# Weights of a decoder block's FFN through shared buffers, and the first three down tiles in another order

## The chip, the cores and the metric

One NeuronCore of a Trainium2 chip runs the whole kernel. The time is device microseconds of one execution, the median of several; the profile is that of one execution, with times counted from the start of its span. Engines are named PE (TensorE), DVE (VectorE), ACT (ScalarE), POOL (GpSimd) and SP (SyncE, which issues the DMAs here).

## The reference, cut to what matters

One layer of a decoder, fp32, 1024 tokens of 1024 channels:

```python
h = x
h = h + token_mixer(rms_norm(h, norm_mix))              # three branches, merged, @ w_mix_out
h = h + cross_attention(rms_norm(h, norm_ca), mem_n)    # 4 heads, 256 memory tokens
hn = rms_norm(h, norm_ffn)
u = causal_dwconv(hn @ ffn_up, ffn_conv_w) + ffn_conv_b # 2 x 2816 columns, width 3 over tokens
gate, val = split(u, 2)
h = h + (silu(gate) * val) @ ffn_down                   # 2816 x 1024
out = rms_norm(h, norm_final)
```

## The kernel before, in words

Every fp32 factor of a product is split into a high and a low part, and a product is three matmuls: high by high, high by low, low by high. A weight or an activation therefore passes four steps before PE can use it: a load into a raw buffer, a cast on ScalarE (high), a subtraction on DVE or GpSimd (low), and then the matmuls. `split_tile` (L233) does this for a weight, in two halves, `pair` (L1483) for a tile of hidden values.

The stream h lives in SBUF as eight tiles h0 to h7 of 128 tokens by 1024 channels. The program runs in stages. The token mixer ends with the merge: `accumulate` (L1079) multiplies activations by rows of a weight for each of the eight token tiles and adds the result to h on DVE (L1097); with `add=False` ScalarE copies it into h instead (L1100). Then `norm_T` (L202) normalises h for the cross-attention: a square with a row sum on ScalarE (L191), some short steps, a scale on DVE (L219), transposes on PE (L225), cast and subtraction (L230, L231). `q_proj` (L1160), `attend` (L1177) and `accumulate` follow for each of four heads.

The FFN's up projection uses a fast scheme for 2 x 2 blocks: the token tiles, even and odd, and the halves of the channels form the blocks. `operands` (L1321) builds the block operands b11, b21, b22 and t1 to t4 from the transposed tiles; `put` (L1306) writes an operand's high and low part, and the low parts of t1, t3 and t4 are GpSimd's (`POOL_T`). For each of 22 hidden tiles f, the loop at L1439 loads four raw weight blocks a11, a12, a21, a22 of the gate and value columns (`raw`, L1411, six raw buffers), forms four sums of them on GpSimd (`wsum`, L1417), splits seven weights (`parts`, L1423), and runs seven products of 12 matmuls (`product`, L1343; 84 matmuls instead of 96). Sums of products make the gate's and the value's columns in four tiles of h (`places`, L1362): even f use h0, h4, h1, h5, odd f h2, h6, h3, h7, since h itself was stored to HBM in `normed` (L1295). The convolution (`conv`, L1431) takes one step on ScalarE and two on DVE, then SiLU (L1461) and a multiply on GpSimd (L1463), and the hidden tile is stored (L1464). The first products of tiles 0 and 1 use weights made ahead, during the cross-attention (`early_parts`, L1285); hidden tile 0 and down row 0 are fetched ahead by `early_pair` (L1399) when f is 14.

The down projection starts at L1502: hidden 0 by down row 0 for the eight token tiles in the order 4, 0, 1, 5, 3, 7, 6, 2, written into h; then hidden 1 and 2 for all tiles, with the residual h loaded and added on GpSimd (`residual`, L1478); then groups of 3, 3, 3, 4 and 4 hidden tiles, and the final norm and the store of the output with the last.

A scheduler puts the instructions of each engine into one order ahead of time, by program order and the offsets of `tc.high_priority`. Each engine works through its order in turn, so a waiting instruction holds those behind it; SP's queue of DMA issues too. SBUF comes from pools, opened and closed like a stack, and a tile in a place that another tile held waits for that tile's last reader. PSUM is two buffers `pd` (1024 columns) and four `pq` (512).

## Time and profile before

| | |
|---|---|
| runs | 2342.14, 2349.14, 2349.61 us; median 2349.14 |
| profiled execution | 2349.42 us, its span 2347.7 us |
| PE busy | 2213.9 us, 94% of the span |
| DVE, ACT, POOL busy | 1443.4, 896.5, 593.6 us |
| mean granted clock of TensorE | 0.975 |

The span is the time from the first to the last instruction, and 1.7 us of the execution lie outside it. A row of a timeline gives the start in the span, the length, the engine, the line, the operation and the tiles written and read; in brackets stands how long the engine had been idle and what ended that. A row that ends in "x3" holds three instructions. The granted clock is TensorE's share of full speed in a stretch. The merge ends at 1345 us, the up loop's last product at 2074 us.

### The profile page before, as it was taken

Reading aid. Unit: us, or ns where it says so; the run is one execution under the profiler, and the core shown is the slowest. Engines: PE = TensorE matmul, PEld = TensorE weight load, DVE = VectorE, ACT = ScalarE, POOL = GpSimd, SP = SyncE. Lnnn points to the kernel's source line nnn. Section 1 sums busy time; section 2 is a strip of 40 time slices with the busy share of each in tenths; the row PEclk is TensorE's granted clock in tenths of the full one; section 3 lists DMA queues with packets and bytes.
Section 4 is the critical chain, followed back from the end, with each engine's and each line's share of the span. In section 5 each row is a group of like instructions: output and inputs, shape, how many; then the busy total and the mean of one; then the engine's idle time right before and its main releaser. Section 6 shows DMA issues by size and latency. Waiting matters only on the chain. (4 is left out here: it accounts for less than half of the span.)

```text
span 2347.7 us, 30015 instructions
## 1 busy us (share of the span) xinstructions
PE 2213.9 (94%) x11635; PEld 1839.8 (78%) x11635; DVE 1443.4 (61%) x1948; ACT 896.5 (38%) x1494; POOL 593.6 (25%) x501
## 2 busy tenths in 40 slices
PE   6999999999999999999999989997899999978998
PEld 5888888878888888887877777875678888867887
DVE  7575555673245245447866565548788888866535
ACT  6644233343434244445521253226444444341212
POOL 2124322222323233221121100004644444313000
PEclk9999989999999999999999999998899999989999
DMA  4334623532211222116664120112222222154311
GB/s 159 117 108 169 204 84 116 146 89 83 81 54 46 90 64 62 64 64 211 217 233 173 63 63 27 32 36 99 91 80 90 82 89 81 55 187 140 116 32 72
DMA packets 232223, 238.93 MB, mean 102 GB/s; under 512 B 35347, under 2 KB 190225, under 8 KB 231057
## 3 DMA queue, kind: packets, MB, share of 16 engines
q1 hardware_dynamic: 232081, 237.02, 31.2%
q8 instruction: 91, 1.49, 0.3%
q14 instruction: 51, 0.42, 0.1%
HBM read 170.92 MB, written 66.06 MB: 101 GB/s over the span
## 5 line engine op out<-in xcount | busy, mean ns | idle before, releaser
L244 ACT CAST wh<-wr 128x512 fp32r<-128x512 f32 x266 | 156.9, 620 | 357.9 <-PE pd L1095 114.7
L245 POOL TENSOR_TENSOR wl<-wr,wh 128x512 fp32r<-128x512 f32 x128 | 177.7, 1405 | 260.4 <-ACT wh L244 246.7
L1097 DVE TENSOR_TENSOR h<-pd,h 128x1024 f32<-128x1024 f32 x120 | 146.3, 1222 | 149.9 <-PE pd L1095 149.8
L284 PE MATMUL pd<-xn_hi,wh 128*128 128x512 f32 x576 | 227.7, 395 | 0.0
L285 PE MATMUL pd<-xn_lo,wh 128*128 128x512 f32 x576 | 225.0, 391 | 0.0
L288 PE MATMUL pd<-xn_hi,wl 128*128 128x512 f32 x576 | 178.4, 391 | 0.0
L266 PE MATMUL pd<-xn_lo,wh 128*128 128x512 f32 x384 | 151.9, 396 | 0.0
L265 PE MATMUL pd<-xn_hi,wh 128*128 128x512 f32 x384 | 151.8, 395 | 0.0
L245 DVE TENSOR_TENSOR wl<-wr,wh 128x512 fp32r<-128x512 f32 x138 | 102.5, 765 | 64.2 <-ACT wh L244 63.1
L938 DVE TENSOR_TENSOR_SCAN B<-B 128x128 f32<-128x128 f32 (+3 forms) x64 | 86.9, 1358 | 84.5 <-POOL B L935 84.1
L1428 DVE TENSOR_TENSOR wp<-ws,wp 128x512 fp32r<-128x512 f32 x88 | 119.8, 1362 | 13.9 <-ACT wp L1427 13.3
L288 PEld LDWEIGHTS pd<-xn_hi,wl 128*128 128x128 f32 x576 | 108.0, 188 | 23.6 <-POOL wl L245 0.2
L285 PEld LDWEIGHTS pd<-xn_lo,wh 128*128 128x128 f32 x576 | 108.4, 188 | 19.8
L284 PEld LDWEIGHTS pd<-xn_hi,wh 128*128 128x128 f32 x576 | 108.2, 188 | 19.5
L269 PE MATMUL pd<-xn_hi,wl 128*128 128x512 f32 x384 | 121.4, 394 | 0.0
L1346 PE MATMUL pq<-t,wp 128*128 128x512 f32 x264 | 103.8, 393 | 16.5 <-ACT wp L1427 16.5
L1463 POOL TENSOR_TENSOR h<-h,h 128x1024 f32<-128x1024 f32 x22 | 56.4, 2564 | 203.3 <-ACT h L1461 171.3
L955 DVE TENSOR_TENSOR al<-pq,ah 128x512 fp32r<-128x512 f32 x80 | 54.6, 688 | 85.6 <-ACT ah L954 85.2
L1427 ACT CAST wp<-ws 128x512 fp32r<-128x512 f32 x88 | 54.4, 618 | 129.5 <-POOL ws L1420 73.9
L1348 PE MATMUL pq<-t,wp 128*128 128x512 f32 x264 | 103.7, 393 | 0.0
L1347 PE MATMUL pq<-t,wp 128*128 128x512 f32 x264 | 103.7, 393 | 0.0
L954 ACT CAST ah<-pq 128x512 fp32r<-128x512 f32 x80 | 46.9, 588 | 145.9 <-PE pq L950 145.6
(420 smaller groups left out, 5812.8 us busy)
## 6 DMA issues: line engine op xcount, KB each, us to landing
wr<-in_w_comb_dram SPq DMA_DIRECT2D x124, 256.0 KB
raw<-in_ffn_up_dram SPq DMA_DIRECT2D x88, 256.0 KB
gate_d<-ft SPq DMA_DIRECT2D x24, 512.0 KB
hid_d<-h SPq DMA_DIRECT2D x22, 512.0 KB
t<-hid_d SPq DMA_DIRECT2D x21, 512.0 KB
wr<-in_ffn_down_dram SPq DMA_DIRECT2D x38, 256.0 KB
wr<-in_ca_wkv_dram SPq DMA_DIRECT2D x32, 256.0 KB
ft<-gate_d SPq DMA_DIRECT2D x16, 512.0 KB
```

Of the source, the lines that this page charges most:

```text
L244: s_.copy(hi[:, sl], raw)
L245: (v_ if lo_e == "dve" else g_).tensor_tensor(lo[:, sl], raw, f32(hi[:, sl]), ALU.subtract)
L265: pe.matmul(o, wh(k), xh(k, h), start=k == 0, stop=False)
L266: pe.matmul(o, wh(k), xl(k, h), start=False, stop=False)
L269: pe.matmul(o, wl(k), xh(k, h), start=False, stop=k == nk - 1)
L284: pe.matmul(o, wh(k), xh(k, h), start=k == 0, stop=False)
L285: pe.matmul(o, wh(k), xl(k, h), start=False, stop=False)
L288: pe.matmul(o, wl(k), xh(k, h), start=False, stop=k == nk - 1)
L1097: v_.tensor_tensor(h[i], ps, h[i], ALU.add)
L1346: pe.matmul(ps, wh[:, k, :], xh[:, k, :], start=k == 0, stop=False)
L1347: pe.matmul(ps, wh[:, k, :], xl[:, k, :], start=False, stop=False)
L1428: v_.tensor_tensor(lo, src, f32(hi), ALU.subtract)
```

## The change

The early weights no longer have a pool of their own. The first up weights of tiles 0 and 1, and later hidden 0 and down row 0, go through `wc`, the pool of the query projection's weights, which is opened first and kept to the end. Behind the norm a pool `raw` of four raw tiles is opened, kept to the end too; the pools `wo` and `co` are opened behind it, where they stood ahead of the norm before. In the up loop five of six raw weight blocks take a tile of `raw`, every sixth one of two buffers of the loop's own pool, and the four of tile 0 are loaded during the cross-attention. `normed` uses its result tile as scratch, of which there are two instead of three. The operands of the last token tiles and the first products alternate in another way. A hidden tile is stored one tile later, behind the next tile's first sums. In the down projection `soon` fetches hidden 1, 2 and down rows 1, 2 in halves through `raw`; tiles 4, 0, 1, 5 take hidden 0, then 1 and 2; then tiles 3, 7, 6, 2 take all three. The residual comes with the next group, of two hidden tiles, and the raw halves of all later down rows pass through `raw`.

```diff
+SOON = 250
-GROUPS = (2, 2, 3, 3, 3, 4, 4)
+GROUPS = (2, 3, 3, 3, 4, 4)
...
-        def split_tile(pl, src, shape, lo_e="dve", tag="w", parts=2, rbufs=3):
+        def split_tile(pl, src, shape, lo_e="dve", tag="w", parts=2, rbufs=3,
+                       rpool=None):
...
-                raw = pl.tile([P, n] + list(shape[2:]), F32, name=tag + "r", bufs=rbufs)
+                if rpool:
+                    raw = rpool.tile([P, 4, P], F32, name="raw").rearrange("p a t -> p (a t)")
+                else:
+                    raw = pl.tile([P, n] + list(shape[2:]), F32, name=tag + "r", bufs=rbufs)
...
-        early = pool(est, "early")
+        early = wp = pool(est, "wc", 2)
         with ExitStack() as st:
-            wo = pool(st, "wo", 2)
-            op = pool(st, "co", 2)
             s3 = ExitStack()
-            wp = pool(s3, "wc", 2)
...
                     norm_T(np_, h, gb, hh, hl, 1)
+            rawp = pool(est, "raw", 4)
+            wo = pool(st, "wo", 2)
+            op = pool(st, "co", 2)
...
-            first = [[early_parts(kh, f) for kh in range(2)] for f in range(2)]
+            rawn, wu = [], []
+
+            def raw(kh, c):
+                rawn.append(0)
+                if len(rawn) % 6 < 5:
+                    t = rawp.tile([P, 4, P], F32, name="raw")
+                else:
+                    t = wu[0].tile([P, 4, P], F32, name="raw", bufs=2)
...
+            first = []
+            for f in range(2):
+                w = split_tile(early, up[:, :, f * P:(f + 1) * P], [P, KD, P], lo_e="pool", rbufs=1)
+                first.append([(w[0][:, k:k + 4, :], w[1][:, k:k + 4, :]) for k in (0, 4)])
+            raw0 = raws(0)
...
-                xs = np_.tile([P, D], F32, name="xs", bufs=3)
+                xs = np_.tile([P, D], F32, name="xs", bufs=2)
+                rs = rms(np_, h[i], xs)
...
-            done = []
-            for f in range(2):
-                done.append(even_products(*first[f]))
-                for _ in range(1 + f):
-                    operands(*todo.pop(0))
+            done = [even_products(*first[0])]
             operands(*todo.pop(0))
-            for f in range(2):
-                even_sums(f, *done[f])
+            done.append(even_products(*first[1]))
+            operands(*todo.pop(0))
+            even_sums(0, *done[0])
+            operands(*todo.pop(0))
+            even_sums(1, *done[1])
+            operands(*todo.pop(0))
...
-                t = wp.tile([P, 4, P], F32, name="raw", bufs=6)
...
+            def store(f):
+                if f >= 0:
+                    dma(hid_d[f], places(f)[0])
...
-                a11, a12 = raw(0, f), raw(1, f)
-                a21, a22 = raw(0, NF + f), raw(1, NF + f)
+                a11, a12, a21, a22 = raws(f) if f else raw0
                 if f >= 2:
                     even_sums(f, *even_products(parts(a11), parts(a12)))
+                store(f - 1)
...
-                dma(hid_d[f], t0)
...
+            def soon(src, tag):
+                hi, lo = tag
+                for sl in (slice(0, 512), slice(512, 1024)):
+                    raw = rawp.tile([P, 4, P], F32, name="raw").rearrange("p a t -> p (a t)")
+                    with tc.high_priority(offset=SOON + 300):
+                        dma(raw, src[:, sl])
+                    with tc.high_priority(offset=SOON):
+                        s_.copy(hi[:, sl], raw)
+                        v_.tensor_tensor(lo[:, sl], raw, f32(hi[:, sl]), ALU.subtract)
+                return hi, lo
...
+            tt = top_tile()
+            tops = [(tt[:, 2 * x], tt[:, 2 * x + 1]) for x in range(4)]
+            w3 = [(d0[0], d0[1])]
+            for x, k in enumerate((1, 2)):
+                w3.append([soon(src[k], tops[2 * x + y]) for y, src in enumerate((hid_d, down))])
+            last()
+            a3, b3 = [w[0] for w in w3], [w[1] for w in w3]
+            accumulate(None, a3[:1], b3[:1], add=False, order=(4, 0, 1, 5))
+            accumulate(None, a3[1:], b3[1:], order=(4, 0, 1, 5))
+            accumulate(None, a3, b3, add=False, order=(3, 7, 6, 2))
...
-                if gi == 0:
-                    ws = [pair(None, hp2.tile([P, T], F32, name="t", bufs=3), down[k], x[1])
-                          for k, x in zip(ks, tiles[2:])]
-                    accumulate(None, [d0[0]], [d0[1]], add=False, order=(4, 0, 1, 5, 3, 7, 6, 2))
-                    gbf = bcast_row(hp2, A["norm_final"][None, :], "gbf")
-                    accumulate(None, acts, ws, after=residual)
-                else:
-                    accumulate(wp, acts, [down[k] for k in ks],
-                               after=final if f == NF else None)
+                accumulate(wp, hidden(ks, tiles), [down[k] for k in ks],
+                           after=final if f == NF else residual if gi == 0 else None, rpool=rawp)
```

Lines of the kernel after the change are 1 to 27 higher for the same statement (L1097 becomes L1103, L1100 L1106, L1420 L1427, L1309 L1327, L1434 and L1436 L1441 and L1443). The orders below are read out of both programs; tiles carry their numbers.

DVE at the end of the merge. h6 and h7 are token tiles whose last sum (L1097, now L1103) ends the merge; ss, rs, rt and xs belong to the norm of a tile, mk and mv to the key and value tiles of the first head. Before:

```order
L1097 TENSOR_TENSOR h6_10567<-pd_11420,h6_10567 128x1024
L1097 TENSOR_TENSOR h7_10568<-pd_11434,h7_10568 128x1024
L192 TENSOR_SCALAR ss_11477<-ss_11477 128x1
L192 TENSOR_SCALAR ss_11488<-ss_11488 128x1
L196 RECIPROCAL rs_11480<-rt_11481 128x1
L196 RECIPROCAL rs_11491<-rt_11492 128x1
L197 SCALAR_TENSOR_TENSOR rt_11481<-rs_11480,ss_11477 128x1
```

With the change:

```order
L1196 TENSOR_TENSOR mv_lo_11834<-kvr_11831,mv_hi_11833 128x512
L200 TENSOR_TENSOR rs_11617<-rs_11617,rt_11618 128x1
L232 TENSOR_TENSOR hn_lo_11461<-pq_11626,top_11460 128x4x128
L232 TENSOR_TENSOR hn_lo_11461<-pq_11633,top_11460 128x4x128
L220 SCALAR_TENSOR_TENSOR xs_11651<-h6_10567,rs_11617,gb_11465 128x1024
L1103 TENSOR_TENSOR h7_10568<-pd_11434,h7_10568 128x1024
L1190 TENSOR_TENSOR mk_lo_12262<-kvr_12259,mk_hi_12261 128x512
L232 TENSOR_TENSOR hn_lo_11461<-pq_11653,top_11460 128x4x128
L232 TENSOR_TENSOR hn_lo_11461<-pq_11660,top_11460 128x4x128
```

The norm's steps stood behind all eight sums; now those of h0 to h6 stand between and ahead of them, and h7's sum comes behind the subtractions of mk and mv.

POOL at the FFN's start. ws are the weight sums of up tile 0, t1, t3 and t4 operands (their low parts), L1340 (now L1358) a difference of two blocks in h. Before:

```order
L1340 TENSOR_TENSOR h4_10565<-h4_10565,h5_10566 128x512
L1309 TENSOR_TENSOR t41_13319<-h4_10565,t40_13318 128x4x128
L1309 TENSOR_TENSOR t11_13313<-h6_10567,t10_13312 128x4x128
L1309 TENSOR_TENSOR t31_13317<-h7_10568,t30_13316 128x4x128
L1340 TENSOR_TENSOR h6_10567<-h6_10567,h7_10568 128x512
L1420 TENSOR_TENSOR ws_13826<-raw_13822,raw_13824 128x512
L1420 TENSOR_TENSOR ws_13828<-ws_13826,raw_13818 128x512
L1309 TENSOR_TENSOR t41_13319<-h6_10567,t40_13318 128x4x128
L1420 TENSOR_TENSOR ws_13848<-raw_13818,raw_13822 128x512
```

With the change:

```order
L1427 TENSOR_TENSOR ws_13817<-raw_13349,raw_13351 128x512
L1427 TENSOR_TENSOR ws_13819<-ws_13817,raw_13345 128x512
L1427 TENSOR_TENSOR ws_13839<-raw_13345,raw_13349 128x512
L1327 TENSOR_TENSOR t41_13318<-h4_10565,t40_13317 128x4x128
L1327 TENSOR_TENSOR t11_13312<-h6_10567,t10_13311 128x4x128
L1358 TENSOR_TENSOR h6_10567<-h6_10567,h7_10568 128x512
L1327 TENSOR_TENSOR t31_13316<-h7_10568,t30_13315 128x4x128
L1427 TENSOR_TENSOR ws_13892<-raw_13347,ws_13819 128x512
L1327 TENSOR_TENSOR t41_13318<-h6_10567,t40_13317 128x4x128
```

The first two weight sums moved ahead of four operand steps, of h4, h6 and h7, the third ahead of five.

DVE where the up loop ends. L1360 (now L1378) are the last sums of up tile 21, L1434 and L1436 (L1441, L1443) its convolution in h2 and h6, L1493 and L245 (L1505, L250) low parts of hidden tiles and down rows, L1103 a sum into h. Before:

```order
L1360 TENSOR_TENSOR h3_10564<-pd_16856,h6_10567 128x4x128
L1434 SCALAR_TENSOR_TENSOR h2_10563<-h3_10564,prf_103,h2_10563 128x1023
L1436 SCALAR_TENSOR_TENSOR h2_10563<-h3_10564,prf_103,h2_10563 128x1022
L1493 TENSOR_TENSOR top_16929<-t_16930,top_16929 128x1024
L1493 TENSOR_TENSOR top_16929<-t_16934,top_16929 128x1024
L1493 TENSOR_TENSOR top_16929<-t_16938,top_16929 128x1024
L1493 TENSOR_TENSOR top_16929<-t_16942,top_16929 128x1024
L1434 SCALAR_TENSOR_TENSOR h6_10567<-h7_10568,prf_103,h6_10567 128x1023
L245 TENSOR_TENSOR wl_17160<-wr_17162,wh_17161 128x512
L1436 SCALAR_TENSOR_TENSOR h6_10567<-h7_10568,prf_103,h6_10567 128x1022
L245 TENSOR_TENSOR wl_17160<-wr_17166,wh_17161 128x512
```

With the change:

```order
L1378 TENSOR_TENSOR h3_10564<-pd_16847,h6_10567 128x4x128
L250 TENSOR_TENSOR wl_17135<-raw_17137,wh_17136 128x512
L250 TENSOR_TENSOR wl_17135<-raw_17141,wh_17136 128x512
L1441 SCALAR_TENSOR_TENSOR h2_10563<-h3_10564,prf_103,h2_10563 128x1023
L1443 SCALAR_TENSOR_TENSOR h2_10563<-h3_10564,prf_103,h2_10563 128x1022
L1441 SCALAR_TENSOR_TENSOR h6_10567<-h7_10568,prf_103,h6_10567 128x1023
L1443 SCALAR_TENSOR_TENSOR h6_10567<-h7_10568,prf_103,h6_10567 128x1022
L1505 TENSOR_TENSOR al_17125<-t_17123,ah_17124 128x1024
L1103 TENSOR_TENSOR h4_10565<-pd_16985,h4_10565 128x1024
L250 TENSOR_TENSOR wl_17145<-raw_17151,wh_17146 128x512
L1103 TENSOR_TENSOR h0_10561<-pd_16999,h0_10561 128x1024
```

The four convolution steps stand together, and the low parts of hidden 1, 2 and down 1, 2 (L1516) stand ahead of these rows, among the earlier sums of up tile 21.

## Rows read from the trace of the kernel before

**Rows 1.** Windows of 50 us: stretch, length, busy PE, PEld, DVE, ACT, POOL (instructions), PEclk, DMA.

```profile
1350.00:1400.00 50.00, 42.49 (x208) 34.93 (x209) 34.27 (x73) 25.80 (x53) 0.00 (x0) 0.89 0.25 74
1600.00:1650.00 50.00, 28.64 (x140) 23.25 (x138) 38.59 (x67) 29.51 (x58) 26.50 (x20) 0.81 0.22 74
1650.00:1700.00 50.00, 44.49 (x179) 35.56 (x178) 42.98 (x43) 22.39 (x32) 27.62 (x18) 0.92 0.33 103
1750.00:1800.00 50.00, 50.00 (x222) 41.42 (x221) 44.73 (x47) 22.32 (x30) 21.86 (x12) 1.00 0.25 82
2050.00:2100.00 50.00, 40.67 (x163) 31.85 (x162) 27.73 (x31) 22.73 (x26) 7.94 (x2) 0.88 0.46 163
2100.00:2150.00 50.00, 41.39 (x168) 32.49 (x167) 35.15 (x27) 11.02 (x14) 21.31 (x8) 0.95 0.57 189
```

**Rows 2.** Timeline of PE, 1350 to 1361: start, length, line, operation, [idle before].

```profile
1351.34 3.43 PE L225 MATMUL pq<-ident,xs 128*128 128x128 f32 x16 [6.10 <-DVE ss L192]
1356.37 1.06 PE L225 MATMUL pq<-ident,xs 128*128 128x128 f32 x8 [1.60 <-DVE xs L219]
1360.52 1.94 PE L225 MATMUL pq<-ident,xs 128*128 128x128 f32 x8 [3.08 <-DVE ss L192]
```

**Rows 3.** Timeline of ScalarE at the end of the merge.

```profile
1345.27 1.06 ACT L191 ACTIVATE junk<-h 128x1024 f32<-128x1024 f32 x1 [27.52 <-PE pd L1095]
```

**Rows 4.** Timeline of PE, 1649 to 1669, the first up tiles.

```profile
1649.38 0.79 PE L1346 MATMUL pq<-t,wp 128*128 128x512 f32 x1 [16.50 <-ACT wp L1427]
1668.71 0.77 PE L1346 MATMUL pd<-b,wp 128*128 128x512 f32 x1 [5.50 <-DVE h L1360]
```

**Rows 5.** Timeline of GpSimd (POOL), 1646 to 1650.

```profile
1646.07 1.26 POOL L1420 TENSOR_TENSOR ws<-raw 128x512 f32<-128x512 f32 x1
1648.63 1.27 POOL L1309 TENSOR_TENSOR t<-h,t 128x512 fp32r<-128x512 f32 x1
```

**Rows 6.** Timeline of PE, 2090 to 2136, the down projection begins.

```profile
2091.33 0.79 PE L1091 MATMUL pd<-ew 128*128 128x512 f32 x1 [6.61 <-ACT h L1100]
2096.45 0.80 PE L1091 MATMUL pd<-top 128*128 128x512 f32 x1 [2.19 <-ACT h L1100]
2135.96 0.75 PE L1091 MATMUL pd<-wh,ah 128*128 128x512 f32 x1 [4.99 <-DVE h L1097]
```

**Rows 7.** Timelines of SP (issues) and ScalarE, 1375 to 1379.

```profile
1375.14 0.34 SPq L1180 DMA_DIRECT2D kvr<-mk_d  x1
1378.17 0.62 ACT L1183 CAST mk_hi<-kvr 128x512 fp32r<-128x512 f32 x1 [0.25 <-DMA kvr<-mk_d]
```

**Rows 8.** Timelines of ScalarE, DVE and GpSimd, last up tile.

```profile
2085.31 1.24 ACT L1432 ACTIVATE h<-h,prf 128x1024 f32<-128x1024 f32 x1
2088.39 1.28 DVE L1436 SCALAR_TENSOR_TENSOR h<-h,prf,h 128x1022 f32<-128x1022 f32 x1
2089.81 5.54 POOL L1463 TENSOR_TENSOR h<-h,h 128x1024 f32<-128x1024 f32 x1 [25.30 <-DVE h L1436]
```

**Rows 9.** Timelines of DVE, GpSimd and ScalarE, 2109 to 2135.

```profile
2122.84 1.23 DVE L1097 TENSOR_TENSOR h<-pd,h 128x1024 f32<-128x1024 f32 x1 [1.49 <-PE pd L1095]
2126.71 8.07 DVE L1493 TENSOR_TENSOR top<-t,top 128x1024 fp32r<-128x1024 f32 x3
2119.93 13.76 POOL L1481 TENSOR_TENSOR h<-h,hr 128x1024 f32<-128x1024 f32 x5 [0.40 <-DMA hr<-h_d]
2109.47 0.62 ACT L244 CAST wh<-wr 128x512 fp32r<-128x512 f32 x1 [2.40 <-DMA wr<-in_ffn_down_dram]
```

**Rows 10.** Lines of GpSimd, 1740 to 2050; then timelines, ScalarE and PE.

```profile
L1420 POOL TENSOR_TENSOR ws<-raw 128x512 f32<-128x512 f32 x32 | 53.8, 1682 | 1.3
L1463 POOL TENSOR_TENSOR h<-h,h 128x1024 f32<-128x1024 f32 x17 | 40.8, 2402 | 156.9 <-ACT h L1461 156.9
2047.83 0.63 ACT L1427 CAST wp<-ws 128x512 fp32r<-128x512 f32 x1 [3.04 <-POOL ws L1420]
2071.16 0.39 PE L1346 MATMUL pd<-b,wp 128*128 128x512 f32 x1
```

53 lines of the change are left out of this document (23 added, 30 removed).

## The prediction

> **What bounds the kernel now.** I read the table of windows first [rows 1]. Its PE column is the engine's busy time in 50 us: from 1750 to 2050 every window is full at a granted clock of 1.00, so nothing in the up loop can be won but fewer matmuls, and the change keeps their number. PE is short in three places only: 42.5 of 50 us from 1350 (the norm ahead of cross-attention), 28.6 and 44.5 from 1600 (the operands of the FFN), 40.7 and 41.4 from 2050 (from the up loop into the down projection). The granted clock is lower in the same windows (0.81 to 0.95, means of stretches at 2.4 and at 1.2 GHz), and each of them holds gaps, so an idle microsecond there costs a little more than itself. Then the PE timeline of each place, for the gaps in brackets and the engine that ended them, and after it the timeline of that engine.
>
> At the norm PE waits 6.10, 1.60 and 3.08 us [rows 2] (two smaller gaps add 1.5), because ScalarE's first square starts only at 1345.27, after the last matmul of the merge, having been idle for 27.52 us [rows 3], while the sums of h0 to h6 were ready one by one, every 2.72 us, before that. At the FFN's start PE waits 16.50 us for a weight's cast and 5.50 us for a sum [rows 4]; GpSimd has one chain there, and the first two weight sums stand at its end, at 1646.07 [rows 5]. At the down projection the gaps are 6.61, 2.19 and 4.99 us [rows 6], with three of 0.8 to 1.5 us between.
>
> **Part 1, the norm.** The norm's buffers no longer lie where they must wait for the merge, so its squares, scales and transposes move in between the last eight sums. What it can give: the 10.8 us of [rows 2] less the tail of h7 (its sum, square, scale and transposes, some 2 us of them before PE can start), 9 us. What it can cost: DVE has the sum (1.23 us [rows 9]), the scale of about the same length and five short instructions for every tile that PE finishes in 2.72 us; that is slightly over PE's pace, and the last sums slip by some 5 us in all. The order also puts the subtractions of the key and value tiles ahead of h7's sum, and such a load took 3.0 us from its issue at 1375.14 to its cast at 1378.17 [rows 7]. If that load is waited for in full where nothing covers it, the place loses 3 us. Going down the new order with these durations I find h7's last transposes at about 1371.5, where the key load, which waits for them today, went out at 1375.14 [rows 7]. I take **-4 us** (between +3 and -9).
>
> **Part 2, the FFN's start.** On GpSimd the first two weight sums now stand ahead of four operand steps that they followed, the third ahead of five. The product that waited 16.50 us needs the first two sums, its cast and the operand t2; what it gains is bounded by the four steps that are passed, at 1.27 us each [rows 5], so some 5 us and, with 2 us of the second gap, 7. But the low part of t3's last piece now comes after all three (3.8 us), and t3's product stands right behind t2's on PE. The work that GpSimd has in all is the same. So part of the 16.50 goes and part comes back at the next product; at worst the three sums delay t3 by 3 us more than t2 gains. The 5.50 us gap is the same chain one tile on, and moves with it. Going down the order: PE restarts at about 1647.4 instead of 1649.38, and the second gap is about 1 us shorter. I take **-3 us** (+3 to -7). The first up weights, loaded through the query projection's buffers and with raw tiles ahead, I cost at nothing: they are hidden by the attention of the last head, in which PE was not waiting for a load; without that cover a load of 3 us [rows 7] would show once.
>
> **Part 3, the down projection.** Output tiles 3, 7, 6 and 2 are written where the last up tile (f=21) has its sums. Today the product with hidden 0 runs over all eight tiles, 48 matmuls or 10.9 us at 0.227 us (some 220 in a full window [rows 1]), and then stands: f=21's value half gets its convolution late, behind casts (ScalarE 2085.31, DVE until 2089.67), and GpSimd's multiply, which frees h6, runs from 2089.81 for 5.54 us [rows 8], where it takes 2.40 in the loop [rows 10]. The loss: from the end of the last up product (2071.16 plus 12 matmuls, 2073.9 [rows 10]) to 2135.96 there are 62.1 us, in which 169 matmuls ran, 38.3 us; so 23.8 us went, 18 of it in gaps and the rest at the lower clock.
>
> After the change tiles 4, 0, 1, 5 take hidden 0, 1 and 2 first: 24 + 48 matmuls, 16.3 us, to 2090.2. The order places the four convolution steps together (4 x 1.25 us), so they end at about 2082, the multiply follows, 2.4 to 5.5 us, and the store of hidden 21 is needed only for tile 2, the last. So 3, 7, 6, 2 find their places free, and the 72 matmuls left end at about 2107.8 (1 us of gaps). Today the same 144 were done at about 2125.4 (the gap of 4.99 began at 2130.97 and the next group had run 24 matmuls, 5.6 us). That is 17.6 us.
>
> What is late next is the residual: it still comes in GpSimd's five adds of the next group. Beside them DVE's three subtractions took 8.07 us, 2.7 each instead of 1.23, and the adds 13.76, and behind these stands the sum that PE waited 4.99 us for [rows 9, 6]. The Trainium skill ("GPSIMD Engine Reference", section Specifications) says that GpSimd's SBUF interface is shared with VectorE, and that an instruction with two SBUF inputs contends. By it the gap stays, since the subtractions read both operands from SBUF, and the part gives 17.6; were it only late data, the gap would go with earlier loads and the part would give 22.6. The trace agrees with the rule: beside the same adds DVE's sums, which read one operand from PSUM, kept their 1.23 us [rows 9]. I leave the gap where it is, and take off one more of the size of those that a sum of DVE ended before (1.5 us), since the four weights of that group now come through four raw tiles. I take **-16 us**: at most -23 (all that was lost but one microsecond), at least -8 (the gaps after 2100, 8.6 us, come a second time).
>
> The eight half loads of hidden 1, 2 and down 1, 2, with 8 casts and 8 subtractions (0.6 and 0.7 us), stand before f=21's sums on ScalarE and DVE, 5 us on each. Their cover: the last weight of the up loop was cast at 2047.83 and used at 2071.16 [rows 10], so both engines have 23 us in which PE needs only evacuations, and the tiles go in after 2060, when the last product that reads that place is over. Without the cover f=21's sums, and with them PE, would be late by up to those 5 us. The deferred store of a hidden tile frees SP's queue and costs nothing while nothing reads it for 20 us.
>
> **Sum.** -4 - 3 - 16 = -23 us, on the profiled execution's 2349.42 us: **2326.4 us**. (That execution is 0.28 us above the median of the three runs.) 7 us, 0.3%, is about what can be told from no change.
>
> **Rivals.**
> 1. *The down projection keeps half its gaps* (16%). For: the weights now come in 256 KB halves through four raw tiles; ScalarE's order has up to six casts ahead of the copy that empties PSUM for tile 3, and a cast that waits for its load holds that copy. Today such casts waited up to 2.40 us each for their loads [rows 9]. Against: these loads go out 20 us earlier. Price: -8 there, and -1 each in the other places: 2339. (The Trainium skill, "DMA: Bandwidth & Descriptors", section Bandwidth, wants transfers of 1 MiB or more, which speaks against cutting 512 KB in two; no run here shows the loss.)
> 2. *The raw ring starves the up loop* (6%), the case that ends slower. Place: 1750 to 2050. Now six raw tiles, each in its turn; then five of six come from four tiles, and the second pair of a tile can be loaded only when the last weight sum of the tile before has read its own. The round is then a load (3.0 [rows 7]), four weight sums (4 x 1.68) and the multiply (2.40) [rows 10], 12.1 us. It decides once it is over the 19.03 us of a tile, so if loads or waits in SP's queue add 7 us. At 20.5 us, 20 tiles lose 29 us, and with the gains of the other parts the time is 2355. Against: the 7 us, and weights that lie ready 23 us ahead.
> 3. *The change doesn't do what it says* (7%): norm and FFN give back what they win (the slipped sums, the passed operands), and the down projection saves only the 6.61: 2343 to 2350, no change.
> 4. *Everything moves by its upper bound* (9%): -9, -5, -22: 2313.
>
> **How the numbers follow.** The forecast has 62%, by itself 2317 to 2336. Faster by over 0.3%: forecast, rivals 1 and 4, 0.87; the same 0.07; slower 0.06. The range takes in the forecast, most of rival 1 and half of rival 4: 2313 to 2341.
>
> **What would show it.** Right: a first square of the norm ended by DVE, not by PE, near 1325; the gap before the first product of up tile 0 of 13 to 15 us; no gap over 2 us between the end of the up loop and the residual's group, and the granted clock at 1.00 through it; PE full from 1750 to 2050 as before. Wrong: gaps on PE in the up loop that a raw tile's load ends (rival 2); copies that end late behind casts with a DMA as releaser after 2075 (rival 1); a gap of over 8 us at the end of the merge.

## The result, and the profile after

The changed kernel takes 2313.22 us in the median of four runs (2307.97 to 2318.63), the kernel before 2349.38 us in the median of four on the same chip: a ratio of 0.9848, with a 95% interval of 0.9813 to 0.9883. It is faster by 36 us, where 23 were forecast; the time lies at the low edge of the range. The profiled execution took 2312.78 us, its span is 2311.1 us, and TensorE's mean granted clock rose from 0.975 to 0.982.

The table of windows of the changed kernel, which answers to [rows 1] and has its columns; from the FFN's start on everything happens some 18 to 36 us earlier than in the kernel before, so that these windows don't hold quite the same work:

```profile
1350.00:1400.00 50.00, 48.71 (x254) 39.29 (x253) 32.70 (x64) 22.61 (x48) 0.00 (x0) 1.00 0.34 100
1600.00:1650.00 50.00, 27.07 (x106) 21.08 (x105) 37.66 (x48) 22.85 (x43) 37.18 (x26) 0.70 0.18 53
1650.00:1700.00 50.00, 47.95 (x208) 39.01 (x208) 43.33 (x43) 23.16 (x32) 24.43 (x15) 0.99 0.30 95
1750.00:1800.00 50.00, 50.00 (x222) 41.44 (x221) 43.50 (x47) 22.30 (x30) 21.31 (x13) 1.00 0.24 78
2050.00:2100.00 50.00, 47.34 (x206) 37.93 (x204) 33.77 (x36) 25.02 (x32) 5.72 (x2) 1.00 0.66 217
2100.00:2150.00 50.00, 48.52 (x206) 39.67 (x207) 27.80 (x25) 6.50 (x11) 18.86 (x7) 0.97 0.37 124
```

The norm's window is nearly full now (48.7 of 50 us, clock 1.00 where it was 0.89), the up loop is full as before, and both windows of the down projection have lost most of their gaps. The FFN's start looks worse (27.1 us, clock 0.70), but mostly because the window now begins later in it: from 1579 to 1629, which is 21 us earlier, PE is busy for 30.5 us at 0.81, about as before.

Which part gave what is read best from stages that can be cut in every profile at the same instruction. These rows group PE's matmuls by line and operands, with the first and the last start of each group:

```profile
L1101 PE MATMUL pd<-wh,ml x128: 388/389/628, 1226.9 to 1343.5; 128*128 128x512 f32 x128
L1101 PE MATMUL pd<-wh,ol x128: 387/389/479, 1414.2 to 1593.8; 128*128 128x512 f32 x128
L1101 PE MATMUL pd<-top x32: 387/389/395, 2062.7 to 2090.2; 128*128 128x512 f32 x32
```

```profile
L1366 PE MATMUL pd<-b,wp x88: 388/389/632, 1648.4 to 2055.3; 128*128 128x512 f32 x88
```

The merge is "wh,ml", the output projection of cross-attention "wh,ol"; "b,wp" is the last product of each up tile, and "top" the products with hidden 1 and 2. The columns of the table are: start of the merge; its length; from there to the first output product ("norm": the norm, with the queries and the attention of the first head); to the last one; to the last up product; to the last product of hidden 0 to 2; to the end of the span.

| kernel | merge starts | merge | norm | attention | FFN start, up loop | hidden 0 to 2 | rest |
|---|---|---|---|---|---|---|---|
| before | 1230.4 | 114.4 | 84.3 | 185.6 | 459.0 | 51.4 | 222.6 |
| changed | 1226.9 | 116.6 | 70.7 | 179.6 | 461.5 | 34.9 | 220.9 |
| 1 norm and buffers | 1229.6 | 115.9 | 70.8 | 181.1 | 461.0 | 34.1 | 217.3 |
| 2 norm waits | 1230.9 | 114.4 | 80.6 | 182.6 | 460.9 | 34.9 | 220.9 |
| 3 all tiles | 1232.1 | 116.9 | 70.5 | 181.0 | 460.8 | 35.7 | 217.2 |
| 4 FFN old order | 1234.0 | 116.1 | 70.5 | 181.2 | 460.6 | 34.9 | 220.9 |
| 5 late loads | 1230.0 | 116.3 | 70.6 | 180.9 | 460.9 | 38.1 | 220.7 |
| 6 offset 0 | 1228.1 | 117.1 | 70.6 | 180.9 | 461.8 | 34.9 | 220.9 |
| 7 interleaved | 1228.0 | 115.5 | 70.6 | 181.5 | 461.0 | 34.1 | 217.3 |
| 8 norm filled | 1232.5 | 114.3 | 79.6 | 179.7 | 461.1 | 34.8 | 221.0 |
| 9 both undone | 1220.4 | 116.9 | 70.6 | 179.6 | 462.3 | 43.5 | 217.1 |
| 10 old down | 1233.8 | 116.2 | 70.7 | 179.3 | 462.3 | 49.4 | 216.4 |
| 11 FFN filled | 1226.6 | 116.7 | 70.6 | 181.1 | 467.2 | 34.0 | 217.3 |
| 12 query late | 1229.8 | 114.5 | 84.0 | 183.0 | 461.0 | 34.9 | 220.9 |

The merge starts anywhere from 1220 to 1234 us, though nothing was changed ahead of it: that is the spread of the run times. Where a stage was left alone, the norm and the last two columns repeat within a microsecond and the merge, the attention and the FFN within 2.2, so the stages tell apart what the times can't. From the start of the merge the kernel before needs 1117.3 us, the changed one 1084.2, so 33.1 us come from the change (the other 3.5 from the stage ahead of it): merge and norm 11.4, attention 6.0, FFN -2.5, the down projection 18.2.

These 33.1 us are of two kinds. PE is idle for 25.2 us less; the other 7.9 us are the same matmuls in less busy time, at a higher granted clock. The attention and the FFN show both (the first row of each pair is of the kernel before):

```profile
1429.10:1614.70 185.60, 178.39 (x863) 145.79 (x862) 102.58 (x179) 60.83 (x134) 9.53 (x4) 0.98 0.12 42
1414.20:1593.80 179.60, 174.99 (x863) 143.24 (x862) 99.01 (x173) 61.68 (x137) 14.68 (x8) 1.00 0.15 51
1614.70:2073.70 459.00, 429.67 (x1882) 353.61 (x1881) 389.99 (x422) 190.06 (x271) 222.11 (x129) 0.97 0.26 84
1593.80:2055.30 461.50, 432.58 (x1882) 355.56 (x1881) 390.91 (x436) 197.05 (x283) 211.84 (x129) 0.96 0.26 84
```

PE's timeline at the norm (start, length, line, operation, idle time before and what ended it), which answers to [rows 2], and ScalarE's, which answers to [rows 3]. The first row is of the kernel before, where the query projection begins; it is L259 in the changed kernel:

```profile
1362.29 0.79 PE L254 MATMUL pd<-top,wh 128*128 128x512 f32 x1
1344.87 2.45 PE L226 MATMUL pq<-ident,xs 128*128 128x128 f32 x16 [0.99 <-DVE hn_lo L232]
1348.15 0.50 PE L259 MATMUL pd<-top,wh 128*128 128x512 f32 x1 [0.84 <-ACT top L231]
1363.36 1.06 PE L226 MATMUL pq<-ident,xs 128*128 128x128 f32 x8 [0.29 <-DVE xs L220]
```

```profile
1300.75 0.62 ACT L249 CAST wh<-wr 128x512 fp32r<-128x512 f32 x1 [4.03 <-DMA wr<-in_ca_wq_dram]
1314.42 0.62 ACT L249 CAST wh<-wr 128x512 fp32r<-128x512 f32 x1 [3.52 <-DMA wr<-in_ca_wq_dram]
1324.22 1.06 ACT L192 ACTIVATE junk<-h 128x1024 f32<-128x1024 f32 x1 [9.18 <-DVE h L1103]
```

The first square of the norm comes at 1324.22, 20 us ahead of the end of the merge, and what it waited for is a sum on DVE. PE's gaps are under a microsecond. The casts at 1300.75 and 1314.42 are of the first query weights, which were cast at 1350.15 and later in the kernel before.

The FFN's start, answering to [rows 4]:

```profile
1615.61 1.94 PE L1335 MATMUL pq<-ident,xs 128*128 128x128 f32 x8 [6.83 <-DVE xs L1321]
1627.81 1.22 PE L1364 MATMUL pq<-t,wp 128*128 128x512 f32 x2 [10.26 <-ACT t L1326]
1631.90 1.22 PE L1365 MATMUL pq<-t,wp 128*128 128x512 f32 x2 [2.87 <-POOL t L1327]
1647.56 0.61 PE L1364 MATMUL pd<-b,wp 128*128 128x512 f32 x1 [2.33 <-DVE h L1378]
```

The gap of 16.50 us has become three, 6.83, 10.26 and 2.87 us, where the forecast had one of 13 to 15; all gaps of PE from the last output product to the full up loop sum to 28.9 us, and to 29.3 in the kernel before.

The down projection, answering to [rows 6], and below it the last up tile's convolution and multiply, answering to [rows 8]:

```profile
2058.70 0.50 PE L1097 MATMUL pd<-wh 128*128 128x512 f32 x1 [0.30 <-ACT h L1106]
2068.48 0.50 PE L1097 MATMUL pd<-top 128*128 128x512 f32 x1 [1.06 <-DVE h L1103]
2100.60 0.50 PE L1097 MATMUL pd<-wh,ah 128*128 128x512 f32 x1 [1.90 <-DVE h L1103]
2125.15 0.50 PE L1097 MATMUL pd<-wh,top 128*128 128x512 f32 x1 [0.88 <-DVE h L1103]
```

```profile
2060.74 1.28 DVE L1441 SCALAR_TENSOR_TENSOR h<-h,prf,h 128x1023 f32<-128x1023 f32 x1 [0.35 <-ACT h L1439]
2062.06 1.28 DVE L1443 SCALAR_TENSOR_TENSOR h<-h,prf,h 128x1022 f32<-128x1022 f32 x1
2063.80 2.41 POOL L1474 TENSOR_TENSOR h<-h,h 128x1024 f32<-128x1024 f32 x1 [15.52 <-ACT h L1472]
```

The convolution's last step ends at 2063.34, 7.6 us after the last up product's end (2055.7), where it took 15.6 us before (2089.67 against 2074.1); the multiply takes 2.41 us and not 5.54.

### The profile page after: what moved, and what is told of

It reads as the page before. It is cut to its first block, busy times and chain, and to the rows that moved or that the text cites. A ratio compares the mean times of both kernels' runs of the same rounds, so it can differ in the third digit from the quotient of the medians.

```text
span 2311.1 us, 29979 instructions
## 1 busy us (share of the span) xinstructions
PE 2201.0 (95%) x11635; PEld 1829.7 (79%) x11635; DVE 1429.0 (62%) x1948; ACT 896.7 (39%) x1498; POOL 580.5 (25%) x501
## 5 line engine op out<-in xcount | busy, mean ns | idle before, releaser
L250 POOL TENSOR_TENSOR wl<-wr,wh 128x512 fp32r<-128x512 f32 x136 | 189.3, 1408 | 523.6 <-ACT wh L249 508.3
L249 ACT CAST wh<-wr 128x512 fp32r<-128x512 f32 x236 | 139.4, 621 | 294.8 <-PE pd L271 79.7
L1103 DVE TENSOR_TENSOR h<-pd,h 128x1024 f32<-128x1024 f32 x116 | 141.6, 1221 | 123.5 <-PE pd L1101 123.2
L943 DVE TENSOR_TENSOR_SCAN B<-B 128x128 f32<-128x128 f32 (+3 forms) x64 | 86.9, 1358 | 84.3 <-POOL B L940 83.9
L1435 DVE TENSOR_TENSOR wp<-ws,wp 128x512 fp32r<-128x512 f32 x88 | 113.3, 1288 | 14.1 <-ACT wp L1434 13.7
L250 DVE TENSOR_TENSOR wl<-wr,wh 128x512 fp32r<-128x512 f32 x100 | 73.0, 749 | 55.3 <-ACT wh L249 55.0
L1434 ACT CAST wp<-ws 128x512 fp32r<-128x512 f32 x88 | 54.4, 618 | 133.2 <-POOL ws L1427 76.3
```

Of the source, the lines that this page charges most:

```text
L249: s_.copy(hi[:, sl], raw)
L250: (v_ if lo_e == "dve" else g_).tensor_tensor(lo[:, sl], raw, f32(hi[:, sl]), ALU.subtract)
L1103: v_.tensor_tensor(h[i], ps, h[i], ALU.add)
L1435: v_.tensor_tensor(lo, src, f32(hi), ALU.subtract)
```

## The experiments

All were compared with the kernel before on the same chip; the profiles are in the table of stages.

**1. Norm's place, buffers and early loads alone.** The two orders are set back.

```diff
-            done = [even_products(*first[0])]
...
+            done = []
+            for f in range(2):
+                done.append(even_products(*first[f]))
+                for _ in range(1 + f):
+                    operands(*todo.pop(0))
...
-            accumulate(None, a3[:1], b3[:1], add=False, order=(4, 0, 1, 5))
-            accumulate(None, a3[1:], b3[1:], order=(4, 0, 1, 5))
-            accumulate(None, a3, b3, add=False, order=(3, 7, 6, 2))
+            accumulate(None, a3[:1], b3[:1], add=False, order=(4, 0, 1, 5, 3, 7, 6, 2))
+            accumulate(None, a3[1:], b3[1:])
```

> The changed kernel, with the old order of operands at the FFN's start and the old order of tiles in the down projection (hidden 0 by all eight tiles, then hidden 1 and 2 by all eight). What is left of the change: the place of the norm's buffers, the shared buffers and the early loads. Theory A (the stages of the two profiles: the norm gave some 17 us, not 4, the down tiles some 16, the FFN's order nothing): 2325 to 2331 us. Rival B (the norm gave 4 as forecast, and the rest came with the order of the down tiles and the FFN): 2340 to 2346 us.

Measured: 2311.20 us (2306.96 to 2313.81), ratio 0.9852 (0.9829 to 0.9875). Both theories missed: all of the gain is there without either of the new orders. Neither the order of tiles nor that of the operands is what the change lives on.

**2. The norm waits again.** The pools `raw`, `wo` and `co` are opened ahead of the norm.

```diff
         early = wp = pool(est, "wc", 2)
+        rawp = pool(est, "raw", 4)
         with ExitStack() as st:
+            wo = pool(st, "wo", 2)
+            op = pool(st, "co", 2)
...
-            rawp = pool(est, "raw", 4)
-            wo = pool(st, "wo", 2)
-            op = pool(st, "co", 2)
```

> The changed kernel, with the raw pool and the pools of the output projection opened ahead of the norm, so that the norm's buffers lie again where they wait for the merge; nothing else. Theory A: the first square of the norm is ended by the last matmul of the merge again, PE gets back gaps of some 10 us and a granted clock under 0.9 from 1350 to 1400, and the time is 2327 to 2333 us. Rival B (the norm's start is worth 4 us): 2315 to 2320 us.

Measured: 2324.42 us (2318.81 to 2328.46), ratio 0.9909 (0.9882 to 0.9935). PE's gaps at the norm are back in part:

```profile
1349.96 5.30 PE L226 MATMUL pq<-ident,xs 128*128 128x128 f32 x24 [4.32 <-DVE ss L193]
1358.78 3.65 PE L226 MATMUL pq<-ident,xs 128*128 128x128 f32 x16 [3.52 <-DVE ss L193]
```

ScalarE's first square waits for the last matmul of the merge again, and the granted clock from 1350 to 1400 is 0.89 again. Merge and norm take 195.0 us, against 187.3 with the change and 198.7 before: the norm's start is worth 7.7 us there, and 3.7 us came otherwise. The time lies between the two theories: the norm's start is worth less than A wanted and more than B.

**3. Down projection in the old order of tiles**, the second half of the edit of experiment 1 alone.

```diff
-            accumulate(None, a3[:1], b3[:1], add=False, order=(4, 0, 1, 5))
-            accumulate(None, a3[1:], b3[1:], order=(4, 0, 1, 5))
-            accumulate(None, a3, b3, add=False, order=(3, 7, 6, 2))
+            accumulate(None, a3[:1], b3[:1], add=False, order=(4, 0, 1, 5, 3, 7, 6, 2))
+            accumulate(None, a3[1:], b3[1:])
```

> The changed kernel, with the first three down products in the old order of tiles (hidden 0 by all eight, then hidden 1 and 2 by all eight); the early half loads stay. If the order of the tiles gives the gain: a gap of several us at tile 3, and 2326 to 2332 us. Rival (the early loads and the convolution steps that stand together give it): 2313 to 2318 us.

Measured: 2311.95 us (2308.82 to 2315.91), ratio 0.9853 (0.9828 to 0.9878). The rival holds (the time lies 1 us under its range): the stage of hidden 0 to 2 takes 35.7 us in place of 34.9. The rest is even 3.7 us shorter (217.2): the residual's group waits 0.63 us and not 1.90 and 0.88, which is some 2 us, and the same matmuls take 207.65 us in place of 209.27. The last up tile's convolution ends 7.7 us after the last up product, as with the change.

**4. FFN's start in the old order**, the first half of that edit.

```diff
-            done = [even_products(*first[0])]
...
+            for f in range(2):
+                done.append(even_products(*first[f]))
+                for _ in range(1 + f):
+                    operands(*todo.pop(0))
```

> The changed kernel, with the old order of first products, operands and first sums at the FFN's start. By the stages of the two profiles the new order is worth nothing or costs 2 us: 2309 to 2314 us. Rival (it gives 3 us, as forecast): 2315 to 2318 us.

Measured: 2317.96 us (2310.81 to 2319.98), ratio 0.9877 (0.9851 to 0.9903), which looks like the rival. The stages say otherwise: this profile's merge started 7 us later than the changed kernel's, and from there it takes 1084.2 us, as the changed kernel does. The new order is worth nothing: the gaps of the FFN's start are the same, and the second weight sum ends 30.5 us after the last output product here and 30.6 with the change.

**5. Late loads.** Hidden 1, 2 and down 1, 2 come through `pair`, whole and from the last stage's buffers.

```diff
-                w3.append([soon(src[k], tops[2 * x + y]) for y, src in enumerate((hid_d, down))])
+                w3.append([pair(None, src[k], tops[2 * x + y]) for y, src in enumerate((hid_d, down))])
```

> The changed kernel, with hidden 1 and 2 and down rows 1 and 2 loaded as before (whole tiles through the buffers of the last stage, which are free only after the up loop) in place of the early halves; the new order of tiles stays. Theory C (the early loads give the gain at the down projection, since the last up tile's convolution is then not behind their casts, and the order of the tiles gives nothing): PE waits again, the 144 matmuls of hidden 0 to 2 take 45 us or more after the up loop, not 35, and the time is 2322 to 2332 us. Rival (either of the two is enough): 35 to 38 us, and 2312 to 2317 us.

Measured: 2319.57 us (2313.24 to 2327.05), ratio 0.9887 (0.9857 to 0.9918). In the stage 38.1 us, 3.2 more than with the early loads; PE waits for the tiles' casts, a little each time, as in

```profile
2065.85 0.50 PE L1097 MATMUL pd<-top 128*128 128x512 f32 x1 [0.70 <-ACT top L1504]
2070.73 0.73 PE L1097 MATMUL pd<-top 128*128 128x512 f32 x2 [1.05 <-ACT top L1504]
```

So theory C falls too, and the rival holds by the stage but for 0.1 us, though not by the time: the convolution ends 14.3 us after the last up product, nearly as late as before, but with the new order of tiles that does little harm.

**6. Early loads without the high offset.**

```diff
-SOON = 250
+SOON = 0
```

> The changed kernel with the offset of the early halves set from 250 to 0: they are loaded early still, but their casts and subtractions take their place in program order. If the place in ScalarE's and DVE's order counts, the convolution of up tile 21 is late and the stage takes 40 us or more for its 144 matmuls: 2318 to 2328 us. If the early data is what counts: 35 to 37 us and 2311 to 2317 us.

Measured: 2315.98 us (2313.96 to 2319.20), ratio 0.9871 (0.9856 to 0.9886); the stage is 34.9 us, as with 250. So the size of the offset doesn't matter. But this run doesn't test whether the place counts: with 0, too, all eight casts and subtractions still stood ahead of the convolution, which ended 7.7 us after the last up product in both.

**7. Token tiles interleaved**, on the kernel of experiment 1, so that GpSimd's operand work can start earlier.

```diff
-                if len(todo) > LAG and todo[0][0] % 2 == 0:
+                if len(todo) > LAG:
...
-            accumulate(wo, o, wrows, after=after, rbufs=2, order=(0, 2, 4, 6, 1, 3, 5, 7))
+            accumulate(wo, o, wrows, after=after, rbufs=2, order=(0, 2, 1, 4, 3, 6, 5, 7))
```

> A version that should beat both: the kernel of the first experiment (norm's place, shared buffers, early loads, old orders elsewhere), and the token tiles of the last output projection in the order 0, 2, 1, 4, 3, 6, 5, 7 in place of 0, 2, 4, 6, 1, 3, 5, 7. GpSimd's 16 operand steps of the odd tiles, 5.1 us for each tile, can start two tiles (5.4 us) earlier, so if they bound the FFN's start, the stage from the last output projection to the end of the up loop falls by 4 to 8 us, from 461 us: 2303 to 2309 us. If DVE bounds it as much, the sums of the output projection come late instead: no change, 2310 to 2315 us.

Measured: 2311.31 us (2309.69 to 2315.84), ratio 0.9853 (0.9836 to 0.9869). The stage keeps its 461.0 us. The second weight sum ended 27.8 us after the last output product in place of 30.5, but the first product came no earlier (34.5 us in place of 34.0). The wait just ahead of it fell from 10.20 to 3.94 us, and others took its place:

```profile
1608.66 1.94 PE L1335 MATMUL pq<-ident,xs 128*128 128x128 f32 x8 [3.64 <-DVE ss L193]
1630.10 0.49 PE L1364 MATMUL pq<-t,wp 128*128 128x512 f32 x1 [3.94 <-ACT t L1326]
1648.63 0.77 PE L1364 MATMUL pd<-b,wp 128*128 128x512 f32 x1 [4.72 <-DVE h L1378]
```

**8. The norm's gaps filled.** The kernel of experiment 2, with 68 transposes that nothing reads, so that it computes more than it needs.

```diff
+                if len(xts) == NT and not on_pool:
+                    for x in range({0: 9, 3: 8}.get(t, 0)):
+                        ps = PQ()
+                        for j in range(4):
+                            pe.transpose(out=ps[:, j * P:(j + 1) * P],
+                                         in_=xts[NT - 1][:, j * P:(j + 1) * P], identity=ident)
```

> The kernel of the second experiment, in which the norm waits for the merge, with 68 more transposes of h7 into PSUM that nothing reads, in the two long gaps of PE at the norm (36 ahead of the first tile's, 32 ahead of the fourth's). The gaps stay, so what the time falls by is the granted clock. Theory (of the 10 us at the norm some 4 are the clock): granted clock 0.9 or more from 1350 to 1370 instead of 0.7, and the stage from the end of the merge to the first output projection 76 to 78 us instead of 80.6. Rival (the gaps alone count): 80 to 82 us.

Measured once: 2324.66 us. The windows of 10 us at the norm:

```profile
1340.00:1350.00 10.00, 8.68 (x45) 7.11 (x44) 4.79 (x13) 4.51 (x8) 0.00 (x0) 1.00 0.16 54
1350.00:1360.00 10.00, 8.57 (x75) 7.83 (x74) 9.39 (x28) 9.44 (x22) 0.00 (x0) 1.00 0.00 1
1360.00:1370.00 10.00, 9.63 (x63) 8.08 (x61) 9.60 (x24) 4.46 (x10) 0.00 (x0) 1.00 0.01 2
```

The granted clock stays at 1.00 where it was 0.67 and 0.76. The norm's stage fell by 1.0 us only, so the forecast of the stage was missed. The attention's fell by 2.9, 1.2 of it in gaps and 1.7 in busy time at a clock of 1.00 in place of 0.99; but that clock is 0.99 in some profiles and 1.00 in others of kernels that don't differ there (180.9 to 181.5 us against 179.3 to 179.7), so the 2.9 can't be put down to the fill. The time is that of experiment 2, with more work. A single profile shows this.

**9. Both undone:** the edits of experiments 3 and 5 together.

```diff
-                w3.append([soon(src[k], tops[2 * x + y]) for y, src in enumerate((hid_d, down))])
+                w3.append([pair(None, src[k], tops[2 * x + y]) for y, src in enumerate((hid_d, down))])
...
-            accumulate(None, a3[:1], b3[:1], add=False, order=(4, 0, 1, 5))
...
+            accumulate(None, a3[:1], b3[:1], add=False, order=(4, 0, 1, 5, 3, 7, 6, 2))
```

> The changed kernel with both the old order of tiles and the late loads of hidden 1, 2 and down rows 1, 2; what stays of the change at the down projection is the ring of raw tiles for the later down rows and the groups. Theory D (either of early loads and tile order is enough, and both undone bring the old gaps back): the 144 matmuls of hidden 0 to 2 take 45 to 52 us after the up loop in place of 35, a copy or a sum of 5 us or more ahead of tile 3, and 2322 to 2330 us. Rival (the gain came with the ring for the later weights, whose loads no longer wait for the up loop's end and whose casts no longer stand in the convolution's way): 34 to 39 us, 2311 to 2317 us.

Measured: 2319.48 us (2312.07 to 2320.50), ratio 0.9884 (0.9860 to 0.9908). The stage takes 43.5 us, and the old gap is back:

```profile
2068.33 0.80 PE L1097 MATMUL pd<-wh 128*128 128x512 f32 x1 [7.44 <-ACT h L1106]
```

Theory D holds in kind, though the stage is 1.5 us and the time 2.5 us short of its ranges: the early loads alone save 8 to 9 us of the stage (experiments 3 and 1), the order of tiles alone 5 (experiment 5), and both undone lose them. The convolution ends 15.6 us after the last up product, as in the kernel before.

**10. The old down projection:** experiment 9 with the later rows' raw halves in three buffers of the last stage.

```diff
-            wp = pool(st, "wd", 7)
+            wp = pool(st, "wd", 6)
...
-                           after=final if f == NF else residual if gi == 0 else None, rpool=rawp)
+                           after=final if f == NF else residual if gi == 0 else None)
```

> The kernel of the run before, with the raw halves of the later down rows in buffers of the last stage as before (three of them), not in the ring; six weights in place of seven in that stage, for room. By theory D it is the same as the run before, within 3 us. By the rival the old stage comes back only here: 45 to 52 us, 2322 to 2330 us.

Measured: 2327.36 us (2325.58 to 2329.78), ratio 0.9922 (0.9899 to 0.9944). 49.4 us in the stage, 6 more than with the ring: the rival has a part, too. 3.3 us of these are gaps, 2.6 the lower clock (0.86 in place of 0.92). The stage also has one weight buffer fewer here, which was not tried apart.

```profile
2079.91 0.79 PE L1097 MATMUL pd<-wh 128*128 128x512 f32 x1 [6.58 <-ACT h L1106]
2085.07 0.80 PE L1097 MATMUL pd<-top 128*128 128x512 f32 x1 [2.23 <-ACT h L1106]
```

```profile
2078.43 5.54 POOL L1474 TENSOR_TENSOR h<-h,h 128x1024 f32<-128x1024 f32 x1 [25.32 <-DVE h L1443]
```

This is the kernel before again (gaps of 6.61 and 2.19, a multiply of 5.54). With the ring the multiply of experiment 9 took 2.66 us.

**11. The FFN's gaps filled**, on the kernel of experiment 1, with 144 transposes that nothing reads.

```diff
+            def fill(n, xs):
+                for _ in range(n):
+                    ps = PQ()
+                    for j in range(4):
+                        pe.transpose(out=ps[:, j * P:(j + 1) * P],
+                                     in_=xs[:, j * P:(j + 1) * P], identity=ident)
...
+            fill(14, xl)
...
+            fill(22, xl)
```

> The kernel of the first experiment (a little shorter than the changed one by its stages), with 144 more transposes of normalised tiles into PSUM that nothing reads, in the two long gaps of PE at the FFN's start (6.8 and 10.2 us). The gaps stay; if the granted clock of 0.5 behind them costs what its windows show (some 4 to 6 us over the matmuls that run at 0.5 to 0.66), the granted clock there is 0.9 or more, the stage from the last output projection to the end of the up loop is 455 to 458 us instead of 461, and the time is 2305 to 2309 us. If the chain of operands and weights sets the end of this stage whatever the clock, it stays 460 to 462 us and the time 2309 to 2314 us.

Measured: 2313.90 us (2308.95 to 2315.45), ratio 0.9863, longer by 6 us in its stage (467.2), which neither side had expected. The granted clock was 1.00 in most windows there. But this is not the kernel of experiment 1 with its gaps filled: GpSimd's order came out another, with the first weight sums behind the last operand steps. The second sum ended 39.8 us after the last output product in place of 30.5, and the product waited for its weight's cast, 1.4 us after the fill had ended:

```profile
1632.14 1.27 POOL L1438 TENSOR_TENSOR ws<-raw 128x512 f32<-128x512 f32 x1
1623.90 10.18 PE L1408 MATMUL pq<-ident,xs 128*128 128x128 f32 x76 [1.76 <-ACT h L1350]
1635.46 0.50 PE L1364 MATMUL pq<-t,wp 128*128 128x512 f32 x1 [1.38 <-ACT wp L1445]
```

So this run doesn't tell what the clock costs at the FFN's start; that stays open.

**12. The query weights late.** The kernel of experiment 2, with the raw buffer of the query weights held until the merge has ended.

```diff
+            held = wp.tile([P, 4, P], F32, name="wr", bufs=1)
+            with tc.high_priority(offset=600):
+                s_.copy(held.rearrange("p a c -> p (a c)"), h[NT - 1][:, 0:512])
```

> The kernel of the second experiment (norm waits for the merge), with the query weights' raw buffer held by a copy of half of h7 until the merge has ended (one ScalarE copy of 0.6 us more), so that the first query weights are loaded and cast beside the norm, as in the kernel before, in place of 30 to 45 us ahead of it. From the end of the merge to the last output product the kernel before took 269.9 us and the second experiment 263.2. If the early query weights gave these 6.7 us: 267 to 272 us, and 2327 to 2333 us for the whole. Rival (they came from the first up weights and the raw tiles in the shared buffers): 262 to 265 us, and 2322 to 2327 us.

Measured: 2329.10 us (2326.05 to 2332.29, seven runs), ratio 0.9931 (0.9912 to 0.9950). The gaps of the kernel before (6.10, 1.60 and 3.08 us [rows 2]) return within half a microsecond:

```profile
1350.34 3.62 PE L226 MATMUL pq<-ident,xs 128*128 128x128 f32 x16 [5.65 <-DVE ss L193]
1355.42 1.07 PE L226 MATMUL pq<-ident,xs 128*128 128x128 f32 x8 [1.46 <-DVE xs L220]
1359.76 1.94 PE L226 MATMUL pq<-ident,xs 128*128 128x128 f32 x8 [3.27 <-DVE ss L193]
```

Merge and norm take 198.5 us, as before (198.7), and 195.0 in experiment 2: the early query weights are the other 3.5 us. The attention's stage did not follow (183.0 against 185.6 before); with it the theory is met at its lower edge (267.0 us), and the time lies in its range.

## Why the prediction was right, and where it was not

**Part 1 was right in its mechanism and far too small:** -4 us at the norm, and nothing for the buffers behind it; measured 11.4 in merge and norm and 6.0 in the attention. The step that failed is "going down the new order with these durations I find h7's last transposes at about 1371.5", 3.6 us earlier. Counted from the start of the merge, they ended 7.2 us earlier (137.5 us after it in place of 144.7), and they were not what PE had to wait for: it began the query projection, with tiles that were done before h7, 121.2 us after the start of the merge in place of 131.9, and that covered h7's tail. Of the 11.4 us, 8.7 are idle time of PE and 2.8 the same matmuls at a granted clock of 0.98 in place of 0.95. Two terms were mis-sized, and one was left out:

- PE's merge slips by 2.2 us (116.6 against 114.4 us), not 5, though h7's own sum slips by 15 (from 114.9 to 130.1 us after the start of the merge).
- The clock: the text said that an idle microsecond "costs a little more than itself", and put no number to it; it gave the 2.8 us above.
- The query weights were not entered at all, though `wc`, now the first pool, lets them be loaded beside the merge: 3.5 us (experiment 12). The norm's own start is nearly all of the rest, 7.7 (experiment 2).

For the attention's 6.0 us, PE's gaps there are 2.6 us shorter (7.2 and 4.6), and the same 863 matmuls took 3.4 us less busy time, at 1.00 in place of 0.98; what part of the change brought that was not tried apart, and the clock there also differs between profiles of one program (experiment 8). That h7's sum would wait for the load of the keys did not come: it started at 1356.97, 13 us after its last matmul, but DVE had idled only 0.33 us since 1343.70; the subtractions, scales and short steps that its new order puts ahead held it.

**Part 2 was wrong:** -3 forecast, +2.5 measured. PE was to restart "at about 1647.4 instead of 1649.38", 2 us earlier; counted from the last output product it restarted after 34.0 us in place of 34.7. The two weight sums did end earlier, by 3.4 us (30.6 in place of 34.0), with either order (experiment 4). The step that failed is that they, with their casts, end the wait: it ended with the cast of t2, an operand that the working names but doesn't price. ScalarE's order now has the casts of the sums ahead of the last operand casts, so it idled until GpSimd's sums were there, and cast t2 only then:

```profile
1624.39 0.62 ACT L1434 CAST wp<-ws 128x512 fp32r<-128x512 f32 x1 [3.52 <-POOL ws L1427]
1627.14 0.62 ACT L1326 CAST t<-h 128x512 fp32r<-128x512 f32 x1
```

DVE had what t2's cast reads ready at 1623.10. With still earlier sums (experiment 7) the product came no earlier; there ScalarE waited for DVE's steps ahead of t2's cast. DVE, which makes these operands, was 98% busy from 1610 to 1620 in the changed kernel. t3's low part ended the next wait; GpSimd was 99% busy from 1620 to 1630. The gaps sum to the same 29 us in both kernels and in both orders (experiment 4). The +2.5 us are not in the gaps but in the clock: the same 1882 matmuls took 432.58 us in place of 429.67, at 0.96 in place of 0.97; what lowers it there was not tried. That the first up weights and raw tiles cost nothing there was not contradicted.

**Part 3 was the right size, for a reason that is only half of it:** -16 forecast, -18.2 measured. Tiles 3, 7, 6 and 2 did find their places free, the 144 matmuls took 34.9 us (33.9 were forecast), and the residual's gap of 4.99 us shrank to 1.90 and 0.88. But the reason given, that tiles 4, 0, 1, 5 go first, was not needed: experiment 3 does without. What frees the places there is that the last up tile's convolution no longer stands behind casts of 1.06 us and subtractions of 1.23 us that the early halves have made unnecessary: it ends 7.7 us after the last up product with early loads (1, 3) and 15.6 us without (9, 10). Against experiment 9 the early loads alone save 8 to 9 us, the order of tiles alone 5 (experiment 5). The ring for the later rows gives 6 more (9 against 10, so shown only with the two others undone), which the forecast had entered as a cost of 1.5 us. With early loads the order of tiles gives nothing in this stage and costs 3.7 us in the rest (216.4 to 217.3 us in the six experiments with the old order, 220.7 to 221.0 in the seven kernels with the new).

**The contention of the residual's adds** stayed, as the forecast had it, but the wait behind it did not: 4.99 us became 1.90 and 0.88, and with the old order of tiles one of 0.63 (experiment 3), where the subtractions of that place run ahead of the adds. Of DVE's two subtractions here the first, begun just ahead of GpSimd's add, took 1.22 us; the second, begun beside it, took 3.43 and ended 1.1 us after the add. A sum out of PSUM beside the next add took 1.21. That agrees with the rule of the Trainium skill ("GPSIMD Engine Reference", section Specifications) that VectorE's instructions with two SBUF inputs contend with GpSimd's:

```profile
2094.85 1.22 DVE L1505 TENSOR_TENSOR top<-t,top 128x1024 fp32r<-128x1024 f32 x1
2095.02 3.31 POOL L1492 TENSOR_TENSOR h<-h,hr 128x1024 f32<-128x1024 f32 x1 [28.81 <-DVE h L1103]
2095.99 3.43 DVE L1505 TENSOR_TENSOR top<-t,top 128x1024 fp32r<-128x1024 f32 x1
2100.62 3.30 POOL L1492 TENSOR_TENSOR h<-h,hr 128x1024 f32<-128x1024 f32 x1 [2.29 <-DVE h L1103]
2101.60 1.21 DVE L1103 TENSOR_TENSOR h<-pd,h 128x1024 f32<-128x1024 f32 x1
```

**The rivals.** The ring didn't starve the up loop: PE is full from 1750 to 2050. Casts did wait for their loads at the down projection (up to 5.54 us at 2073.23), but no copy that PE needed stood behind them. The fourth rival, everything at its upper bound, gave the nearest time, and for the wrong sum: -9, -5 and -22 where -17.4, +2.5 and -18.2 were found. That the range held is in part luck: part 1 gave 13.4 us more than was forecast, part 2 5.5 less, part 3 2.2 more, and 3.5 came from ahead of the merge.

**A version beside it.** Experiments 1 and 7, 2311.2 and 2311.3 us, can't be told from the changed kernel's 2313.2 by their times; by the stages they are 4 us shorter, for want of the new order of tiles.

## What to carry to other kernels

Where a buffer lies decides when work may start: opening a pool in another place let a whole norm move under the products ahead of it, and let the next weights load beside them, without a new instruction. When one edit bundles several, undo each alone and also in pairs: two of these were each nearly enough, and undoing one showed little. With a spread of 10 us from a stage that nobody touched, cut the profiles at fixed instructions and compare the stages, not the ends.

## What the runs showed of the hardware

Transposes that nobody reads, put into PE's gaps at the norm, kept the granted clock at 1.00 where it fell to 0.67; the norm's stage, with more work, was 1.0 us shorter (experiment 8, one profile). With the same matmuls, PE's busy time followed the granted clock: 178.39 us at 0.98 and 174.99 at 1.00 in the attention, 429.67 at 0.97 and 432.58 at 0.96 in the FFN. A DVE subtraction of two SBUF operands that began beside a GpSimd add took 3.43 us, one that began ahead of it 1.22. The start of the merge moved between 1220.4 and 1234.0 us in fourteen profiles of kernels that run the same instructions up to there, while the stages behind it repeat within 2.2 us where they were left alone.
